# A hybrid DeltaNet and attention layer: inverse assembly read by ScalarE, layer norm in two VectorE operations a row, gate products in pieces, a later inverse norm

## The chip, the cores and the metric

The kernel runs on one core of one Trainium2 chip. The metric is the device time of one execution in microseconds (us). The engines are TensorE (PE in the rows; its weight loads PEld), VectorE (DVE), ScalarE (ACT), GpSimd (POOL) and SyncE (SP), which issues the DMAs. Each engine works through its own list of instructions in a fixed order and waits on semaphores for the others.

## What is computed

One layer over 2048 tokens of width 1024, float32, with 16 meta tokens in front. Cut to what matters here:

```python
q = l2_normalize(q) * (GDN_DK ** -0.5);  k = l2_normalize(k)
decay = exp(where(tri, g_cum[..., :, None] - g_cum[..., None, :], -inf))
lower = where(strict, einsum('bhnid,bhnjd->bhnij', k * beta, k) * decay, 0)
sol   = triangular_solve(lower + eye(CHUNK), rhs)       # chunks of 64 tokens, 8 heads
attn  = einsum('bhnid,bhnjd->bhnij', q, k) * decay
...                                                     # recurrence over chunks, gated norm
out   = (g_a * (y_a @ w_proj_a) + g_b * (y_b @ w_proj_b)) @ w_out
y     = (h2 - mean(h2)) * rsqrt(var(h2) + LN_EPS) * ln_w + ln_b     # h2 = DEEPNORM_ALPHA * h + out
```

A second branch, sliding-window attention, takes the same input; the change does not touch it.

## The kernel before

The 2048 tokens go in four blocks of 512. For each block the kernel projects the input with all weights, a unit of 16 or 24 matmuls 128x512 at a time (L296; weights as high and low parts wh, wl or wr). Between the units stand the small steps of the DeltaNet branch, in four groups g of two heads each, and then those of the attention branch. A Python scheduler writes this order out at build time: each step is a generator, a `yield` gives way to the next piece of matmuls, `yield 3` inside a background generator means that it goes on three such ticks later. So a different count of yields, or a line at another place, moves instructions in an engine's list, and nothing is reordered on the chip.

The steps of one group, in the names of the rows:

- `conv_unit`: ScalarE copies a projected unit (L681 to L686), VectorE applies a four-tap convolution (three SCALAR_TENSOR_TENSOR of 128x512, L689), ScalarE takes a tanh (L692), VectorE forms the SiLU (L694). This is done for k, q and v of two heads.
- `stage_b0`: GpSimd multiplies a triangle mask with the gate columns gh and gl (L729, one 128x1024 product each), TensorE sums them (L740, two matmuls for each head), ScalarE exponentiates (L741), GpSimd masks (L743). The result is E.
- `stage_b1`: VectorE forms the scalars of the keys (L777 to L781, 128x8) and the lower triangle LT (L784, eight operations reading PSUM). `inverse` then sends its diagonal blocks through DRAM (L798, L802), GpSimd solves them by substitution (62 short L810/L812), and two DMAs bring the result XT back (L818, L823).
- `stage_b2`: the inverse norm irk of the keys (`rsqrt_small` on sk, L160 to L166, and L837: 13 small VectorE operations), then attn = (k q) E (L842 on TensorE, L843 on VectorE) for two heads, the norms of q (L849), then v in token order, which ScalarE scales by irk (L859).
- `stage_c`: XT is transposed (XN, L875) and the inverse is assembled in two levels: L888 on TensorE, Y copied from PSUM (L893), L898/L900, copies into N64 and LT (L901, L904), L909.

At the end of a block, `project` adds the output projection to the residual; the layer norm of its four rows r0 to r3 (128 tokens each) falls into the start of the next block. `norm()` takes mean and inverse deviation for all four rows, then for each row one ScalarE operation (L1278, scale rs and bias nmr = -mean rs), one VectorE product with the weight (L1280), one GpSimd addition of the bias (L1282), and an output DMA on SP (L1284). The last block's rows go through `norm_row` instead. SP also issues the weight loads (L244), in its list's order.

Of the kernel before, what the change touches and what calls it, by code (L numbers as in the profile page):

```python
# [73 lines left out]
def hybrid_kernel(  # L74
# [47 lines left out]
    def g4(shape, dt=F32):  # L122
        return gp.tile(shape, dt, tag="g", name=nm("g"))
# [452 lines left out]
    def block(b, nextx):  # L576
# [145 lines left out]
        def stage_b0(g):  # L722

            d, h0 = gr[g], 2 * g
            yield from until(lambda: "gp" in gates)
            gts = []
            for part in gates["gp"]:
                gt = g4([P, 2, NC4, P], F32R)
                G.tensor_tensor(out=gt, in0=tri.unsqueeze(1).unsqueeze(1).to_broadcast([P, 2, NC4, P]),  # L729
                                in1=part[:, :, h0:h0 + 2].rearrange("p c h -> p h c").unsqueeze(3).to_broadcast([P, 2, NC4, P]), op=ALU.mult)  # L730
                gts.append(gt)
                yield

            def end():
                yield 3
                E = g4([P, 2, TB])
                for hh in range(2):
                    pm = bank()
                    for i, gt in enumerate(gts):
                        T.matmul(pm, strictr, gt[:, hh].rearrange("p c i -> p (c i)"), start=i == 0, stop=i == 1)  # L740
                    A.activation(E[:, hh, :], pm, AF.Exp)  # L741
                    yield 1
                    G.tensor_tensor(out=E[:, hh, :].rearrange("p (c i) -> p c i", c=NC4), in0=E[:, hh, :].rearrange("p (c i) -> p c i", c=NC4),  # L743
                                    in1=tri.unsqueeze(1).to_broadcast([P, NC4, P]), op=ALU.mult)
                d["E"] = E

            bg(end())
# [81 lines left out]
        def stage_b2(g):  # L829
# [2 lines left out]
            yield from until(lambda: ("ok", "qT", 1) in d)  # L832
            kT, qT, E, sk = d["kT"], d["qT"], d.pop("E"), d["sk"]
            sq = tiny([P, 2, NC4], "sq")
            irk = tiny([P, 2, NC4], "irk")
            rsqrt_small(irk, sk, [P, 2, NC4], "rs")
            V.tensor_tensor(out=irk, in0=irk, in1=sk, op=ALU.mult)  # L837
            attn = g4([P, 2, NC4, P])
            for hh in range(2):
                pq = bank()  # L840
                for c in range(NC4):
                    T.matmul(pq[:, c * P:(c + 1) * P], kT[:, hh, c * P:(c + 1) * P], qT[:, hh, c * P:(c + 1) * P], start=True, stop=True)  # L842
                V.tensor_tensor(out=attn[:, hh], in0=pq.rearrange("p (c i) -> p c i", c=NC4), in1=E[:, hh, :].rearrange("p (c i) -> p c i", c=NC4), op=ALU.mult)  # L843
                yield
                pq = bank()
                for c in range(NC4):
                    T.transpose(out=pq[:, c * P:(c + 1) * P], in_=qT[:, hh, c * P:(c + 1) * P], identity=ident)
                for c in range(NC4):
                    A.activation(junk, pq[:, c * P:(c + 1) * P], AF.Square, accum_out=sq[:, hh, c:c + 1])  # L849
                yield  # L850
            vtok = g4([P, 2, NC4, P])
            for hh in range(2):
                yield from until(lambda: ("ok", "vT", hh) in d)
# [13 lines left out]
        def stage_c(g):  # L867
# [22 lines left out]
            Y = tiny([P, 8, 32], "Y", 1)  # L890
            for s in range(2):
                bq = 64 * s + 32
                V.tensor_copy(Y[bq:bq + 32], py[bq:bq + 32, 0:256].rearrange("p (m i) -> p m i", m=8))  # L893
            yield
            px = bank()
            for m in range(8):
# [1 line left out]
                    T.matmul(px[a:a + 32, m * 32:m * 32 + 32], Y[bq:bq + 32, m, :], XT[bq:bq + 32, m, :],  # L898
                             start=True, stop=True, tile_position=(bq, a))
                T.matmul(px[32:64, m * 32:m * 32 + 32], XT[32:64, m, :], Y[32:64, m, :], start=True, stop=True, tile_position=(32, 32))  # L900
            V.tensor_copy(N64[32:64, :, 0:32], px[32:64, 0:256].rearrange("p (m i) -> p m i", m=8))  # L901
            for s in range(2):
                a, bq = 64 * s, 64 * s + 32
                A.activation(LT[a:a + 32, :, bq:bq + 32], px[a:a + 32, 0:256].rearrange("p (m i) -> p m i", m=8), AF.Copy)  # L904
# [341 lines left out]
        def project(nx):  # L1246
# [13 lines left out]
            def scale(n, mv):  # L1260

                var = tiny([P, n], "var")
                V.tensor_scalar(out=var, in0=mv[:, :, 1], scalar1=16.0 * LN_EPS, scalar2=None, op0=ALU.add)
                rs = tiny([P, n], "lrs")
                rsqrt_small(rs, var, [P, n], "ln")
                nmr = tiny([P, n], "nmr")
                V.scalar_tensor_tensor(out=nmr, in0=mv[:, :, 0], scalar=-1.0, in1=rs, op0=ALU.mult, op1=ALU.mult)
                return rs, nmr

            def norm():  # L1270
                lw, lb = norm_params()
                mv = tiny([P, NC4, 2], "mv")
                for c in range(NC4):
                    V.bn_aggr(out=mv[:, c, :], in_=bss[c])
                rs, nmr = scale(NC4, mv)
                for c in range(NC4):
                    yield 3
                    A.activation(xr[c], xr[c], AF.Identity, scale=rs[:, c:c + 1], bias=nmr[:, c:c + 1])  # L1278
                    yield 2
                    V.tensor_tensor(out=xr[c], in0=xr[c], in1=lw, op=ALU.mult)  # L1280
                    yield 1
                    G.tensor_tensor(out=xr[c], in0=xr[c], in1=lb, op=ALU.add)  # L1282
                    yield 2
                    SY.dma_start(out=out_[t0 + c * P:t0 + (c + 1) * P, :], in_=xr[c])  # L1284

            def norm_row(c, params):
                lw, lb = params
                mv = tiny([P, 1, 2], "mvr")
                V.bn_aggr(out=mv[:, 0, :], in_=bss[c])
                rs, nmr = scale(1, mv)  # L1290
                for h in range(2):
                    sl = slice(512 * h, 512 * h + 512)
                    A.activation(xr[c][:, sl], xr[c][:, sl], AF.Identity, scale=rs, bias=nmr)
# [192 lines left out]
```

## Time and profile before

| what | value |
|---|---|
| median of 3 runs | 2690.58 us (2689.68 to 2692.38) |
| the profiled execution | 2691.56 us, of which the profile's span is 2689.8 us |
| TensorE busy | 2611.2 us, 97% of the span |
| VectorE busy | 1623.8 us, 60% |
| ScalarE busy | 1220.4 us, 45% |
| GpSimd busy | 783.6 us, 29% |
| chain that ended last, by engine | PE 77%, DVE 12%, ACT 3%, POOL 3%, DMA 2% |

Times in the views run from the span's start. Block 1 begins near 734 us, block 2 near 1381, block 3 near 2029. The chain is followed back from the last instruction, at each step to what released it. An idle time of an engine is put down to the releaser that came last, in square brackets behind a row; "issue" means that the profile shows no releaser.

### The profile page before, as it was taken

The numbers are of one execution on the slowest core, as the hardware profiler recorded it, in microseconds if no ns is written. First come the engines' busy times: TensorE is split into PE (matmuls) and PEld (weight loads), VectorE is DVE, ScalarE is ACT, GpSimd is POOL, SyncE is SP. The second block draws the span as 40 slices with busy tenths as digits, with TensorE's granted clock in tenths as the row PEclk, the third lists the DMA queues.
The fourth block names the chain that finished last, engine by engine and source line by source line (L and its number), as shares of the span: only waits on it lengthen the run. The fifth ranks groups of instructions, "written<-read, shape, count | busy, mean of one in ns | idle before, by whom it ended". The sixth has DMA issues, their size and how long they took to land.

```text
span 2689.8 us, 44101 instructions
## 1 busy us (share of the span) xinstructions
PE 2611.2 (97%) x15308; PEld 2188.4 (81%) x15308; DVE 1623.8 (60%) x4080; ACT 1220.4 (45%) x3214; POOL 783.6 (29%) x1619
## 2 busy tenths in 40 slices
PE   8999999999999999999998999999999999999997
PEld 6777788888877888888887888888888788888885
DVE  6879768743475665762466564675347466476336
ACT  4555546542244544662234554565223455465322
POOL 1544324432055430111116433110103544111022
PEclk9999999999999999999999999999999999999999
DMA  7654556643664454764465445575357545467533
GB/s 245 210 171 159 189 184 187 202 163 99 200 230 141 145 174 142 207 194 146 151 214 178 140 144 171 170 214 174 117 165 232 169 140 152 154 194 213 162 97 128
DMA packets 243374, 461.64 MB, mean 172 GB/s; under 512 B 77992, under 2 KB 136000, under 8 KB 243152
## 3 DMA queue, kind: packets, MB, share of 16 engines
q1 hardware_dynamic: 243152, 458.82, 54.2%
q8 instruction: 122, 2.00, 0.3%
q14 instruction: 100, 0.82, 0.1%
HBM read 379.89 MB, written 78.82 MB: 171 GB/s over the span
## 4 chain that ended last, share of the span: by engine, by line
PE 77%; DVE 12%; ACT 3%; POOL 3%; DMA 2%; issue 2%; SPq 1%; DVEq 0%; ACTq 0%
PE acc L296 54%; DVE s L689 4%; PE ps L1108 2%; PE ps L1073 2%; POOL X L812 1%; POOL tm L810 1%; PE ps L960 1%; PE ps L939 1%; PE ps L928 1%; PE ps L947 1%; PE ps L949 1%; PE ps L1126 1%; PE acc L1367 1%; PE acc L1370 1%; PE acc L1369 1%
## 5 line engine op out<-in xcount | busy, mean ns | idle before, releaser
L296 PE MATMUL acc<-xh,wh 128*128 128x512 f32 x1800 | 740.6, 411 | 0.7 <-ACT wh L261 0.7
L296 PE MATMUL acc<-xl,wh 128*128 128x512 f32 x1800 | 711.2, 395 | 0.0
L296 PE MATMUL acc<-xh,wl 128*128 128x512 f32 x1800 | 479.1, 398 | 0.0
L296 PEld LDWEIGHTS acc<-xh,wh 128*128 128x128 f32 x1800 | 343.0, 191 | 61.4 <-ACT wh L261 1.0
L296 PEld LDWEIGHTS acc<-xl,wh 128*128 128x128 f32 x1800 | 343.6, 191 | 58.6
L296 PEld LDWEIGHTS acc<-xh,wl 128*128 128x128 f32 x1800 | 333.1, 190 | 67.8 <-issue 0.5
L261 ACT ACTIVATE wh<-wr 128x1024 fp32r<-128x1024 f32 (+1 forms) x245 | 258.0, 1053 | 277.6 <-PE acc L296 158.8
L689 DVE SCALAR_TENSOR_TENSOR s<-st,cw,s 128x512 f32<-128x512 f32 x288 | 252.4, 877 | 67.3 <-ACT st L684 59.9
L144 DVE TENSOR_TENSOR wl<-wr,wh 128x1024 fp32r<-128x1024 f32 (+2 forms) x125 | 165.9, 1327 | 157.3 <-ACT wh L261 138.3
L296 PE MATMUL acc<-y,wh 128*128 128x512 f32 x1024 | 250.1, 392 | 0.0
L810 POOL TENSOR_TENSOR tm<-X,g 128x60 f32<-128x60 f32 (+24 forms) x496 | 169.1, 341 | 265.5 <-DMA g<-d 229.3
L296 PEld LDWEIGHTS acc<-y,wh 128*128 128x128 f32 x1024 | 189.1, 188 | 37.3
L296 PE MATMUL acc<-xh,wr 128*128 128x512 f32 x624 | 210.2, 404 | 0.0
L1225 POOL TENSOR_TENSOR g<-g 128x512 f32<-128x512 f32 x32 | 69.9, 2184 | 432.7 <-DVE g L1218 432.7
L812 POOL TENSOR_TENSOR X<-X,tm 128x60 f32<-128x60 f32 (+24 forms) x496 | 178.9, 361 | 38.9
L1218 DVE SCALAR_TENSOR_TENSOR g<-g,acc 128x512 f32<-128x512 f32 x64 | 44.0, 688 | 203.1 <-PE acc L296 202.9
L1054 POOL TENSOR_TENSOR g<-mo,slp 128x32 f32<-128x32 f32 x128 | 41.1, 331 | 390.3 <-DVE mn L1075 364.5
L1110 ACT ACTIVATE s<-ps 104x512 fp32r<-104x512 f32 (+2 forms) x128 | 76.5, 597 | 146.3 <-PE ps L1108 145.3
L296 PEld LDWEIGHTS acc<-xh,wr 128*128 128x128 f32 x624 | 117.1, 190 | 23.3
L692 ACT ACTIVATE s<-s 128x512 f32<-128x512 f32 x96 | 60.4, 629 | 158.1 <-DVE s L689 158.1
L1209 ACT ACTIVATE g<-acc,bg__157 128x512 f32<-128x512 f32 x64 | 44.2, 690 | 190.2 <-PE acc L296 189.7
L296 PE MATMUL acc<-y,wl 128*128 128x512 f32 x512 | 129.2, 390 | 0.0
(329 smaller groups left out, 4768.5 us busy)
## 6 DMA issues: line engine op xcount, KB each, us to landing
wr<-in_wfm_dram SPq DMA_DIRECT2D x214, 512.0 KB
wl<-ws SPq DMA_DIRECT2D x165, 512.0 KB
wr<-ws SPq DMA_DIRECT2D x78, 512.0 KB
wh<-ws SPq DMA_DIRECT2D x75, 512.0 KB
ws<-wl SPq DMA_DIRECT2D x68, 512.0 KB
g<-kd SPq DMA_DIRECT2D x240, 96.0 KB
ws<-wh SPq DMA_DIRECT2D x38, 512.0 KB
wr<-in_wo_dram SPq DMA_DIRECT2D x32, 512.0 KB
```

Source lines behind the costliest of these rows:

```text
L144: eng.tensor_tensor(out=out_, in0=src, in1=f(hi), op=ALU.subtract)
L261: A.activation(hi, raw, AF.Copy)
L296: T.matmul(ps, w_[:, k, :], r_(k), start=(n == 0), stop=(n == 3 * NK - 1))
L689: V.scalar_tensor_tensor(out=acc, in0=st[:, 3 - d:TB + 3 - d], scalar=cw[:, s, 3 - d:4 - d], in1=acc, op0=ALU.mult, op1=ALU.add)
L692: A.activation(th, acc, AF.Tanh, scale=0.5)
L810: G.tensor_tensor(out=tm[:, :n, :r], in0=X[:, :n, j:j + 1].to_broadcast([P, n, r]), in1=L[:, j:j + 1, j + 1:].to_broadcast([P, n, r]), op= ...
L812: G.tensor_tensor(out=X[:, :n, j + 1:], in0=X[:, :n, j + 1:], in1=tm[:, :n, :r], op=ALU.add)
L1073: T.matmul(o_, d["q", rt][:, 2 * cp2 + ch], KX[:, l, ch, s:208], start=l == 0, stop=l == 1)
L1108: T.transpose(out=pT[0:kt, j * 256 + rt * P:j * 256 + rt * P + P], in_=Pt[:, ch, rt, s + j * kt:s + j * kt + kt], identity=ident)
L1110: A.activation(ph[0:kt], pT[0:kt], AF.Copy)
L1209: A.activation(gt_[u][:, br, :], ps, AF.Tanh, scale=0.5, bias=bg_[:, 8 * br + u:8 * br + u + 1])
L1225: G.tensor_tensor(out=m[:, u % 2, :], in0=t[:, 0, :], in1=t[:, 1, :], op=ALU.add)
```

## The change

Four edits:

1. `stage_b0`: each gate product of 128x1024 becomes four of 128x256 (one head, two of the four chunks).
2. `stage_b2`: the 13 operations of irk move from in front of the attn loop to behind it, in front of vtok.
3. `stage_c`: Y (two copies) and N64's lower block are copied out of PSUM by ScalarE instead of VectorE.
4. `norm()`: a row is now (x - mean) * lw and then x * rs + lb, two VectorE SCALAR_TENSOR_TENSOR of 128x1024; the ScalarE and GpSimd operations go, nmr is formed in `norm_row` only. The yields of a row were 3, 2, 1, 2 and are 1, 1, 1.

```diff
@@ stage_b0
-                G.tensor_tensor(out=gt, in0=tri.unsqueeze(1).unsqueeze(1).to_broadcast([P, 2, NC4, P]),
-                                in1=part[:, :, h0:h0 + 2].rearrange("p c h -> p h c").unsqueeze(3).to_broadcast([P, 2, NC4, P]), op=ALU.mult)
+                for hh in range(2):
+                    for c in range(0, NC4, 2):
+                        G.tensor_tensor(out=gt[:, hh, c:c + 2], in0=tri.unsqueeze(1).to_broadcast([P, 2, P]),
+                                        in1=part[:, c:c + 2, h0 + hh:h0 + hh + 1].to_broadcast([P, 2, P]), op=ALU.mult)
@@ stage_b2
-            irk = tiny([P, 2, NC4], "irk")
-            rsqrt_small(irk, sk, [P, 2, NC4], "rs")
-            V.tensor_tensor(out=irk, in0=irk, in1=sk, op=ALU.mult)
             attn = g4([P, 2, NC4, P])
...
+            irk = tiny([P, 2, NC4], "irk")
+            rsqrt_small(irk, sk, [P, 2, NC4], "rs")
+            V.tensor_tensor(out=irk, in0=irk, in1=sk, op=ALU.mult)
             vtok = g4([P, 2, NC4, P])
@@ stage_c
-                V.tensor_copy(Y[bq:bq + 32], py[bq:bq + 32, 0:256].rearrange("p (m i) -> p m i", m=8))
+                A.activation(Y[bq:bq + 32], py[bq:bq + 32, 0:256].rearrange("p (m i) -> p m i", m=8), AF.Copy)
...
-            V.tensor_copy(N64[32:64, :, 0:32], px[32:64, 0:256].rearrange("p (m i) -> p m i", m=8))
+            A.activation(N64[32:64, :, 0:32], px[32:64, 0:256].rearrange("p (m i) -> p m i", m=8), AF.Copy)
@@ norm
-                    yield 3
-                    A.activation(xr[c], xr[c], AF.Identity, scale=rs[:, c:c + 1], bias=nmr[:, c:c + 1])
-                    yield 2
-                    V.tensor_tensor(out=xr[c], in0=xr[c], in1=lw, op=ALU.mult)
                     yield 1
-                    G.tensor_tensor(out=xr[c], in0=xr[c], in1=lb, op=ALU.add)
-                    yield 2
+                    V.scalar_tensor_tensor(out=xr[c], in0=xr[c], scalar=mv[:, c, 0:1], in1=lw, op0=ALU.subtract, op1=ALU.mult)
+                    yield 1
+                    V.scalar_tensor_tensor(out=xr[c], in0=xr[c], scalar=rs[:, c:c + 1], in1=lb, op0=ALU.mult, op1=ALU.add)
+                    yield 1
                     SY.dma_start(out=out_[t0 + c * P:t0 + (c + 1) * P, :], in_=xr[c])
```

TensorE's list is the same, instruction for instruction. On VectorE, in group 0 of block 1, this stood from the triple L689 to the inverse norm and the attn products (L1280 is row r3 of the norm):

```order
L1280 TENSOR_TENSOR y_7685<-y_7685,y_8020 128x1024
L694 SCALAR_TENSOR_TENSOR g_8509<-s_8498,s_8455 128x512
L689 SCALAR_TENSOR_TENSOR s_8521<-st_8519,cw,s_8521 128x512 x3
L160 TENSOR_SCALAR rsi_8548<-sk_8340 128x8
...
L837 TENSOR_TENSOR irk_8546<-irk_8546,sk_8340 128x8
L843 TENSOR_TENSOR g_8563<-ps_8564,g_8391 128x512
L694 SCALAR_TENSOR_TENSOR g_8509<-s_8577,s_8521 128x512
L655 TENSOR_TENSOR s_8615<-acc_8535,s_8601 128x512
L843 TENSOR_TENSOR g_8563<-ps_8617,g_8391 128x512
```

Now, in the changed kernel (whose L842, L852 are L843, L837 of before):

```order
L694 SCALAR_TENSOR_TENSOR g_8538<-s_8525,s_8483 128x512
L689 SCALAR_TENSOR_TENSOR s_8553<-st_8551,cw,s_8553 128x512 x3
L842 TENSOR_TENSOR g_8577<-ps_8578,g_8421 128x512
L694 SCALAR_TENSOR_TENSOR g_8538<-s_8590,s_8553 128x512
L655 TENSOR_TENSOR s_8628<-acc_8566,s_8614 128x512
L842 TENSOR_TENSOR g_8577<-ps_8630,g_8421 128x512
L655 TENSOR_TENSOR s_8698<-acc_8640,s_8692 128x512
L160 TENSOR_SCALAR rsi_8702<-sk_8371 128x8
...
L852 TENSOR_TENSOR irk_8700<-irk_8700,sk_8371 128x8
```

The row of the norm is gone from here (all eight operations of the norm stand at the block's start), and both attn products stand ahead of the inverse norm.

On ScalarE, at the inverse assembly of the same group (N_275 is N64, L692 the tanh that waits for a triple L689):

```order
L884 ACTIVATE N_275_1550<-XN_8993 32x8x32
L692 ACTIVATE s_9036<-s_8985 128x512
L895 ACTIVATE Y_9055<-ps_9038 32x256 x2
L681 ACTIVATE st_9076<-acc_9015 128x512
L683 ACTIVATE s_9078<-acc_9015,cw 128x512
L684 ACTIVATE st_9076<-carry 128x3
L686 ACTIVATE carry<-st_9076 128x3
L903 ACTIVATE N_275_1550<-ps_9087 32x8x32
```

Y's two copies, which stood on VectorE behind the triple, now stand on ScalarE behind the tanh of the same triple.

On SP, at the start of block 1, before (y_7679 to y_7685 are the rows r0 to r3):

```order
L1284 DMA out_dram<-y_7679 128x1024
L244 DMA wr_8190<-ws_602 128x1024
L244 DMA wr_8191<-ws_603 128x1024
L624 DMA vd<-s_8141 128x512
...
L624 DMA vd<-s_8147 128x512
L244 DMA wh_8273<-ws_696 128x1024
L244 DMA wl_8274<-ws_697 128x1024
L1284 DMA out_dram<-y_7681 128x1024
```

and now (y_7703 to y_7709 are r0 to r3):

```order
L1282 DMA out_dram<-y_7707 128x1024
L244 DMA wr_8218<-ws_608 128x1024
L244 DMA wr_8219<-ws_609 128x1024
L1282 DMA out_dram<-y_7709 128x1024
L624 DMA vd<-s_8166 128x512
...
L624 DMA vd<-s_8172 128x512
L244 DMA wh_8300<-ws_702 128x1024
L244 DMA wl_8301<-ws_703 128x1024
```

The output of all four rows now stands ahead of the value stores (L624) and of the weight pair behind them.

## Rows read from the trace of the kernel before

**Rows 1.** The page, busy us (share of the span) and instructions of each engine.

```profile
PE 2611.2 (97%) x15308; PEld 2188.4 (81%) x15308; DVE 1623.8 (60%) x4080; ACT 1220.4 (45%) x3214; POOL 783.6 (29%) x1619
```

**Rows 2.** The waits of PE: who waited, for whom, us, times, longest.

```profile
PE ps L898 <- issue: 12.5, 3, 4.6
...
PE ps L740 <- DVE g L843: 9.1, 3, 3.1
```

**Rows 3.** Timeline of PE: start, us, line, [idle before it <- releaser]; blocks 0, 1.

```profile
114.98 0.66 PE L760 MATMUL ps<-cm,g 128*128 128x128 f32 x4 [0.95 <-DVE g L694]
...
762.40 0.62 PE L740 MATMUL ps<-g,strictr 128*128 128x512 f32 x2
...
788.87 1.21 PE L740 MATMUL ps<-g,strictr 128*128 128x512 f32 x2 [3.08 <-DVE g L843]
...
831.68 0.67 PE L898 MATMUL ps<-XT,Y 32*32 32x32 f32 x3 [4.26 <-issue]
```

**Rows 4.** Stretches: us, busy time of each engine (instructions), PEclk, DMA share, GB/s.

```profile
788.80:792.30 3.50, 3.43 (x8) 2.70 (x9) 1.82 (x4) 0.65 (x2) 3.14 (x6) 0.52 1.03 411
829.90:836.70 6.80, 4.88 (x57) 3.94 (x58) 6.06 (x14) 3.37 (x8) 0.51 (x2) 0.50 0.59 161
115.00:118.40 3.40, 3.40 (x17) 2.88 (x18) 3.19 (x10) 3.27 (x14) 0.71 (x3) 1.00 0.54 168
```

**Rows 5.** Timeline of DVE in group 0 of block 1, at the attn products.

```profile
781.48 4.28 DVE L689 SCALAR_TENSOR_TENSOR s<-st,cw,s 128x512 f32<-128x512 f32 x3
785.67 0.22 DVE L160 TENSOR_SCALAR rsi<-sk 128x8 int32<-128x8 int32 x1
...
788.13 0.68 DVE L843 TENSOR_TENSOR g<-ps,g 128x512 f32<-128x512 f32 x1
788.74 0.68 DVE L694 SCALAR_TENSOR_TENSOR g<-s,s 128x512 f32<-128x512 f32 x1
```

**Rows 6.** Timeline of POOL in the same stretch.

```profile
780.84 2.78 POOL L1282 TENSOR_TENSOR y<-y,y 128x1024 f32<-128x1024 f32 x1 [6.42 <-DVE y L1280]
...
784.63 0.43 POOL L810 TENSOR_TENSOR tm<-X,g 128x31 f32<-128x31 f32 x1 [0.21 <-DMA g<-d]
...
788.93 1.64 POOL L743 TENSOR_TENSOR g<-g,cm 128x512 f32<-128x512 f32 x1 [1.13 <-ACT g L741]
```

**Rows 7.** Timeline of DVE at the inverse assembly of group 0 of block 1.

```profile
822.42 0.45 DVE L875 STREAM_TRANSPOSE XN<-XT 128x256 f32<-128x256 f32 x1 [3.92 <-DMA XT<-d]
...
823.20 1.54 DVE L779 TENSOR_TENSOR cj<-cj,gm4be 128x8 f32<-128x8 f32 x1
824.77 1.84 DVE L780 TENSOR_SCALAR ncj<-cj 128x8 f32<-128x8 f32 x1
...
828.81 2.32 DVE L689 SCALAR_TENSOR_TENSOR s<-st,cw,s 128x512 f32<-128x512 f32 x3
831.16 0.88 DVE L893 COPY Y<-ps 32x256 f32<-32x256 f32 x2
```

**Rows 8.** Timeline of DVE at the start of block 1.

```profile
735.45 1.23 DVE L1280 TENSOR_TENSOR y<-y,y 128x1024 f32<-128x1024 f32 x1 [1.31 <-ACT y L1278]
738.76 0.42 DVE L611 COPY ba<-acc 128x16 f32<-128x16 f32 x3 [2.09 <-PE acc L598]
...
756.24 2.08 DVE L694 SCALAR_TENSOR_TENSOR g<-s,s 128x512 f32<-128x512 f32 x1 [0.30 <-ACT s L692]
```

**Rows 9.** Timeline of SP at the start of block 1: a weight load.

```profile
748.25 1.00 SPq L244 DMA_DIRECT2D wh<-ws  x1
```

**Rows 10.** Timeline of POOL at 822: the first gate product of a later group.

```profile
822.76 1.94 POOL L729 TENSOR_TENSOR g<-cm,gh 128x1024 fp32r<-128x1024 f32 x1
```

**Rows 11.** The page's costliest groups: busy us, mean ns | idle before, releaser.

```profile
L810 POOL TENSOR_TENSOR tm<-X,g 128x60 f32<-128x60 f32 (+24 forms) x496 | 169.1, 341 | 265.5 <-DMA g<-d 229.3
```

**Rows 12.** Timeline of ACT at the inverse assembly of block 1.

```profile
831.17 0.63 ACT L692 ACTIVATE s<-s 128x512 f32<-128x512 f32 x1 [7.42 <-DVE s L689]
```

**Rows 13.** Timeline of ACT in block 0: v scaled by the inverse norm.

```profile
95.05 1.15 ACT L859 ACTIVATE g<-ps,irk 128x128 f32<-128x128 f32 x4
```

More of the change, by code (lines that the diff above doesn't have):

```diff
@@ L1265, in scale @@
                 rsqrt_small(rs, var, [P, n], "ln")
-                nmr = tiny([P, n], "nmr")
-                V.scalar_tensor_tensor(out=nmr, in0=mv[:, :, 0], scalar=-1.0, in1=rs, op0=ALU.mult, op1=ALU.mult)
-                return rs, nmr
+                return rs
             def norm():
@@ L1274, in norm @@
                     V.bn_aggr(out=mv[:, c, :], in_=bss[c])
-                rs, nmr = scale(NC4, mv)
+                rs = scale(NC4, mv)
                 for c in range(NC4):
-                    yield 3
-                    A.activation(xr[c], xr[c], AF.Identity, scale=rs[:, c:c + 1], bias=nmr[:, c:c + 1])
-                    yield 2
-                    V.tensor_tensor(out=xr[c], in0=xr[c], in1=lw, op=ALU.mult)
                     yield 1
-                    G.tensor_tensor(out=xr[c], in0=xr[c], in1=lb, op=ALU.add)
-                    yield 2
+                    V.scalar_tensor_tensor(out=xr[c], in0=xr[c], scalar=mv[:, c, 0:1], in1=lw, op0=ALU.subtract, op1=ALU.mult)
+                    yield 1
+                    V.scalar_tensor_tensor(out=xr[c], in0=xr[c], scalar=rs[:, c:c + 1], in1=lb, op0=ALU.mult, op1=ALU.add)
+                    yield 1
                     SY.dma_start(out=out_[t0 + c * P:t0 + (c + 1) * P, :], in_=xr[c])
@@ L1289, in norm_row @@
                 V.bn_aggr(out=mv[:, 0, :], in_=bss[c])
-                rs, nmr = scale(1, mv)
+                rs = scale(1, mv)
+                nmr = tiny([P, 1], "nmr")
+                V.scalar_tensor_tensor(out=nmr, in0=mv[:, :, 0], scalar=-1.0, in1=rs, op0=ALU.mult, op1=ALU.mult)
                 for h in range(2):
```

## The prediction

> **What bounds the kernel now.** The page's busy line comes first: TensorE is busy for 2611.2 of 2689.8 us [rows 1], so the other engines matter only where TensorE waits for them, some 60 us in all. The view of TensorE's waits says for whom. Of its long rows, L898 (12.5 us in 3 waits) and L740 (9.1 us in 3) [rows 2] repeat once in each of blocks 1, 2 and 3, in the places that this change edits; the others lie at the start, in block 0 or in the attention half. In block 1 they are L740 at 788.87, after 3.08 us, and L898 at 831.68, after 4.26 us [rows 3]. A wait also costs clock: in the 3.5 us behind the first the granted clock was 0.52, in the 6.8 us around the second 0.50, the 1.2 GHz level, while behind a wait of 0.95 us it stayed at 1.00 [rows 4]. The L740 wait so costs 3.08 + 0.48 x 3.5 = 4.8 us. But gaining those 4.8 us is worth nothing by itself if L898 still begins when it did. So I followed the chain of waits back from L898, and it does not run over TensorE: DVE L689 (781), ACT, POOL L743 (789), POOL's substitution chain L810/L812 to 814.8, two DMAs, XN, the five small operations L777 to L781, L784, L689, Y. **What decides blocks 1 to 3 is how much earlier Y is ready**, until TensorE itself becomes the bound, at 831.68 - 4.26 - 4.8 = 822.6, 9.1 us earlier.
>
> **The norm.** Row r3's L1280 and L1282 leave the front of that chain. The POOL add L1282 lies at 780.84 for 2.78 us, and the three L689 at 781.48 take 4.28 us beside it [rows 5, 6] where a clean triple, at 828.81, takes 2.32 [rows 7]: 2.0 us of that is the POOL add. With L843 no longer behind the inverse norm either, L740's wait goes. Its 4.8 us bring TensorE to L888 at about 819.0, where XN is then late. POOL's next L743 waited 1.13 us for ACT and started at 788.93; the substitution step before it (its first instruction is at 784.63 [rows 6]) was done at 787.8. ACT and DVE being early, L743 starts behind that step, and its DMA comes up to 0.5 us sooner, because the gate pieces let L777 in: the chain begins its rest 1.1 to 1.7 us earlier.
>
> What the norm adds is eight VectorE operations 128x1024 at the block's start, ahead of the gates. Such an operation with a scalar has no row; L1280 takes 1.23 us [rows 8], and at 128x512 a SCALAR_TENSOR_TENSOR like L694 (0.68 us at 788.74) takes as long as a TENSOR_TENSOR (0.68 at 788.13 [rows 5]). Bounds: 1.2 us, and two thirds of a triple of L689, 1.55; I take 1.2. Four of them fill the idle 1.31 us, the place of one L1280 and the 2.09 us in front of L611 at 738.76 [rows 8]. The third row pushes L621 back by 2.0 us and the gates, with half of the fourth row, by 3.1. The other half takes the place of row r1's L1280. The second triple of L689 then loses its POOL add, 2.0 us as at 781, so the gate column gh is about 1.0 us late, at 756.6.
>
> Its DMA: on SP, out row r3 now stands in front of the four value stores L624 and of the weight pair that was issued at 748.25 [rows 9]. r3 is normalised about 753.6, and behind the stores the pair goes at about 755.7, 7 us late. Its matmuls stand right behind L740 at 762.40 [rows 3], another 7 us later. I cost this at nothing; the bounds are 0 and, if the pair needed 9 us, 2.
>
> **The pieces.** L729, 1.94 us for 128x1024 [rows 10], becomes four of 128x256. Bounds for one: a quarter, 0.48, and a quarter plus the 0.34 mean of the small POOL product L810 [rows 11], 0.82; nearest is the quarter, I take 0.55, or 4.4 us for eight. Next to L729 the eight-element L779 took 1.54 us and L780 1.84 [rows 7], each ending with a POOL product, and L694 at 756.24 took 2.08 for 0.68 [rows 8]: VectorE and POOL take turns, instruction by instruction. So with pieces each small operation waits for at most 0.55: L777 to L781 shrink by some 2.0 us. The turns cut the other way too: VectorE gets in between the pieces, and the product as a whole ends later. After XN it then lasts until L689, a triple that was clean at 828.81: one or two pieces fall into it, +0.8 us (0 to 1.65).
>
> The Trainium skill, "SBUF — State Buffer", section "Who interferes with whom", says that a VectorE instruction with two SBUF inputs contends with a GpSimd one that reads SBUF, and that whoever issues first keeps the shared ports for the whole instruction. The elongated rows agree; by that rule alone, a VectorE operation could meet four times as many POOL instructions, which is the second rival's mechanism below.
>
> At the block's start the same turns cost something. gh, 1.0 us late, gives a first piece at 756.9; then L694, three L689 and the pieces alternate, so the sixth piece (which the second L740 needs) ends at 756.9 + 6 x 0.55 + 0.7 + 3 x 0.75 = 763.15, where TensorE asks at about 762.6 [rows 3]: a new wait of 0.5 us, without loss of clock by [rows 4]. It moves the units behind it and so VectorE's input; the chain hides half of it: +0.25.
>
> **Y and N64 on ScalarE.** Y was two copies of together 0.88 us directly behind L689 [rows 7]. On ScalarE they stand behind L692, which starts when L689 is done (831.17, 0.63 us [rows 12]): +0.55 (0 to 0.7). N64 costs nothing: ScalarE was idle then.
>
> **The inverse norm.** 13 operations from 785.67 to 788.13, 2.46 us [rows 5], go behind both L843. In blocks 1 to 3 VectorE has idle time there and nothing is late. In block 0, group 0 it has none: L859 at 95.05 [rows 13] must wait for them, the key-tile copies and L261 queued behind it on ScalarE with it, and through DVE L689 the L760 that waits 0.95 us at 114.98 [rows 3]. Bounds 0 and +2.5; against it, the pieces shorten a wait at 55 and N64 one at 143, about 1.6 us at most. I take +0.8.
>
> **Sum.** Per block 1 to 3: -1.4 (chain) -2.0 (small operations) +0.8 (L689 meets pieces) +0.55 (Y) +0.25 (rest of the new L740 wait that the chain does not hide) = -1.8 us at L898, where all behind it is TensorE-bound. Three blocks -5.4, block 0 +0.8, nothing in the last block's tail: -4.6 us. The profiled execution took 2691.56 us (span 2689.8 and 1.8 around it), 0.98 over the median of 2690.58: 2691.56 - 4.6 - 0.98 = **2686.0 us**.
>
> **The rivals.**
> 1. The chain gives all it can: pieces of 0.48, none left at L689, Y hidden, -3.7 us a block, block 0 even: 2690.6 - 11.1 = 2679.5. For it: TensorE has 9.1 us of room there. Against it: ScalarE's order puts Y behind L692.
> 2. Contention only moves: each L689 of the triple behind XN waits for a piece of 0.55 to 0.8. It takes back 1.65 to 2.0 of the 2.0 us, and with Y's 0.55 only 0.3 us a block are left: 2690.6 - 0.9 + 0.8 = 2690.5. For it: the triples with POOL beside them [rows 5]. Against it: only some of eight pieces are left by then.
> 3. Slower: the second L740 of each block's first group. If a piece costs 0.82 us, the sixth ends 1.6 us later than above, the wait is over 2 us, and the 1.2 GHz level takes a further 1.7 us as behind L740 at 788.87. It decides from about 1 us of wait on, since 0.95 left the clock alone. Then 3.7 us a block arrive at the chain in place of 0.5; nothing is won at L898 but +1.4 to +2: 2690.6 + 5.5 + 0.8 = 2697. An SP queue that hands the weight pair over too late, behind out row r3, would cost at the same place.
>
> **How the numbers follow.** Forecast 0.45 (2682.5 to 2689.5), rival 1 0.20, rival 2 0.17, rival 3 0.15, others 0.03. About 0.2% (5.4 us) is what a measurement of this kernel can tell from no change; the bound is 2685.2. Faster: 0.18 of the forecast, rival 1 and a bit, 0.40. Within: 0.27 of the forecast and most of rival 2, 0.42. Slower: rival 3 and others, 0.18. The range leaves out the ends of rivals 1 and 3: 2678 to 2696.
>
> **What would show it.** Right: L740's wait on DVE L843 gone; a wait at L888 of about 2 us in front of XN; L898 at about 829.9; L777 to L781 within 2 us; Y's first copy behind L692; pieces near 0.55 us; a wait of about 0.5 us at L740 near 762.6. Wrong: an L898 that starts before 828 or after 831, a granted clock of 0.5 behind L740 at 762, TensorE waiting for weights behind out row r3, or time gained outside these places.

## The result, and the profile after

The changed kernel takes 2667.24 us (median of 4 runs, 2665.94 to 2668.51) against 2691.48 us of the kernel before, run beside it: a ratio of 0.9909, interval 0.9897 to 0.992. It is **24 us faster, where 4.6 us were forecast**; the time lies 11 us below the range. The sign of the forecast was right, its size wrong by a factor of five. The profiled execution has a span of 2664.2 us, 25.6 less than before.

The page of the changed kernel, its busy line (us, share of the span, instructions):

```profile
PE 2600.1 (98%) x15308; PEld 2180.1 (82%) x15308; DVE 1587.5 (60%) x4041; ACT 1223.7 (46%) x3250; POOL 765.8 (29%) x1703
```

TensorE is 11 us less busy with the same instructions [rows 1], since it ran less often at half clock (granted clock 0.994 on average, 0.987 before); the rest is waits that went. Its waits now (who, for whom: us, times, longest; line numbers are up by two where code was added above):

```profile
PE ps L900 <- ACT Y L895: 10.2, 8, 3.7
...
PE ps L859 <- ACT g L861: 5.5, 2, 2.8
...
PE ps L890 <- DVE sk L779: 1.3, 1, 1.3
```

L740's wait [rows 2] is gone. L900, the L898 of before, still waits some 10 us [rows 2], but it comes 5 to 7 us earlier in each block. L859 in block 0 waits for v and did not before.

TensorE's list did not change, so each of its 15308 instructions can be set beside its counterpart. L636, early in each block's DeltaNet part, begins 5.3 us earlier in block 1 (744.59 for 749.87), 12.4 in block 2, 19.6 in block 3; the last matmul 25.6. **So block 0 gave 5.3 us, block 1 7.1, block 2 7.2, block 3 with the tail 6.0.** These are one execution of each kernel, and block 0 alone varies: two runs below whose lists are the same in block 0 (irk_first and y_hold) differ there by 5.2 us. What follows counts times in block 1 from L636, which takes out what earlier blocks gave:

| block 1, us behind L636 (lines of the kernel before) | before | after | difference |
|---|---|---|---|
| first keys' operation on sk (L777) | 22.69 | 20.63 | -2.06 |
| LT ready for its DMA (L784 done) | 27.51 | 24.65 | -2.86 |
| substitution begins (L810) | 34.76 | 31.91 | -2.85 |
| GpSimd's next L743 inside it | 39.05 | 34.73 | -4.32 |
| XN (L875) | 72.55 | 67.39 | -5.16 |
| second group's L784 begins | 76.86 | 69.10 | -7.76 |
| triple L689 behind it done | 81.26 | 73.97 | -7.29 |
| L898 | 81.81 | 75.08 | -6.73 |

VectorE at the last rows of this table, in the changed kernel (start us, us, line), beside [rows 7]:

```profile
811.98 0.45 DVE L877 STREAM_TRANSPOSE XN<-XT 128x256 f32<-128x256 f32 x1 [3.58 <-DMA XT<-d]
...
812.75 0.24 DVE L781 TENSOR_TENSOR cj<-cj,gm4be 128x8 f32<-128x8 f32 x1
813.02 0.54 DVE L782 TENSOR_SCALAR ncj<-cj 128x8 f32<-128x8 f32 x1
...
815.77 2.79 DVE L689 SCALAR_TENSOR_TENSOR s<-st,cw,s 128x512 f32<-128x512 f32 x3
```

and ScalarE and TensorE there:

```profile
818.59 0.63 ACT L692 ACTIVATE s<-s 128x512 f32<-128x512 f32 x1 [5.24 <-DVE s L689]
819.24 0.78 ACT L895 ACTIVATE Y<-ps 32x256 f32<-32x256 f32 x2
```

```profile
819.67 0.24 PE L900 MATMUL ps<-XT,Y 32*32 32x32 f32 x2 [2.31 <-ACT Y L895]
```

These last steps went as the forecast had them: the small operations 0.24 and 0.54 us for 1.54 and 1.84, the triple 2.79 for 2.32, Y behind L692. What it missed lies above them in the table, in the front of the chain. There L694 and the first operation on sk stood beside a product before, and now stand beside pieces. Before, and then the changed kernel:

```profile
771.01 1.62 DVE L694 SCALAR_TENSOR_TENSOR g<-s,s 128x512 f32<-128x512 f32 x1 [0.70 <-ACT s L692]
772.56 1.88 DVE L777 TENSOR_SCALAR sk<-sk 128x8 f32<-128x8 f32 x1
```

```profile
764.39 0.90 DVE L694 SCALAR_TENSOR_TENSOR g<-s,s 128x512 f32<-128x512 f32 x1 [0.70 <-ACT s L692]
765.22 0.58 DVE L779 TENSOR_SCALAR sk<-sk 128x8 f32<-128x8 f32 x1
```

GpSimd in the changed kernel, beside [rows 6]: the substitution's first operation, and the L743 of before, which no longer waits.

```profile
776.50 0.64 POOL L812 TENSOR_TENSOR tm<-X,g 128x31 f32<-128x31 f32 x1 [7.50 <-DMA g<-d]
...
779.31 1.30 POOL L745 TENSOR_TENSOR g<-g,cm 128x512 f32<-128x512 f32 x1
```

### The profile page after: what moved, and what is told of

Its sections match the earlier page's. It is cut to its first block, busy times and chain, and to the rows that moved or that the text cites. A ratio compares the mean times of both kernels' runs of the same rounds, so it can differ in the third digit from the quotient of the medians.

```text
span 2664.2 us, 44181 instructions
## 1 busy us (share of the span) xinstructions
PE 2600.1 (98%) x15308; PEld 2180.1 (82%) x15308; DVE 1587.5 (60%) x4041; ACT 1223.7 (46%) x3250; POOL 765.8 (29%) x1703
## 4 chain that ended last, share of the span: by engine, by line
PE 81%; DVE 10%; DMA 3%; POOL 2%; ACT 2%; issue 1%; SPq 1%; DVEq 0%; POOLq 0%; ACTq 0%
PE acc L296 57%; PE ps L1110 2%; DVE s L689 2%; PE ps L1075 2%; PE ps L962 1%; PE ps L941 1%; PE ps L949 1%; PE ps L951 1%; PE ps L930 1%; PE ps L1128 1%; PE acc L1367 1%; PE acc L1370 1%; PE acc L1369 1%; PE ps L841 1%; POOL X L814 1%
## 5 line engine op out<-in xcount | busy, mean ns | idle before, releaser
L689 DVE SCALAR_TENSOR_TENSOR s<-st,cw,s 128x512 f32<-128x512 f32 x288 | 233.4, 810 | 66.6 <-ACT st L684 59.5
L814 POOL TENSOR_TENSOR X<-X,tm 128x60 f32<-128x60 f32 (+24 forms) x496 | 165.4, 333 | 38.9
L731 POOL TENSOR_TENSOR g<-cm,gh 128x256 fp32r<-128x256 f32 x64 | 50.7, 822 | 257.8 <-DVE gh L643 211.5
```

The costliest lines, as they stand in the source:

```text
L689: V.scalar_tensor_tensor(out=acc, in0=st[:, 3 - d:TB + 3 - d], scalar=cw[:, s, 3 - d:4 - d], in1=acc, op0=ALU.mult, op1=ALU.add)
L731: G.tensor_tensor(out=gt[:, hh, c:c + 2], in0=tri.unsqueeze(1).to_broadcast([P, 2, P]), in1=part[:, c:c + 2, h0 + hh:h0 + hh + 1].to_broad ...
L814: G.tensor_tensor(out=X[:, :n, j + 1:], in0=X[:, :n, j + 1:], in1=tm[:, :n, :r], op=ALU.add)
```

## The experiments

Two theories. **"Turns"**: what counts is how long one GpSimd instruction keeps a VectorE operation waiting, all along the chain to L898, so the pieces carry the gain. **"Adds"**: the norm's GpSimd additions beside the triples L689 were what held the chain. All times are medians; the kernel before, run beside each set, had 2690.7, 2690.7, 2691.3 and 2692.3 us.

### Each edit alone

The pieces alone:

```diff
-                G.tensor_tensor(out=gt, in0=tri..., in1=part[:, :, h0:h0 + 2]..., op=ALU.mult)
+                for hh in range(2):
+                    for c in range(0, NC4, 2):
+                        G.tensor_tensor(out=gt[:, hh, c:c + 2], ...)
```

> The kernel before with the gate products in four pieces and nothing else. Theory 'turns': VectorE and GpSimd take turns instruction by instruction, and a whole product of 1.9 us holds up L689, L694 and L777 ahead of the substitution chain as well as L777 to L781 behind it; then pieces alone bring L898 forward by about 5 us in each of blocks 1 to 3 and about 3 us in block 0: 2691.5 - 18 = 2673 us (2670 to 2678). Theory 'adds': the GpSimd additions of the norm are what held the chain; then pieces alone give only the 2 us of L777 to L781 a block: 2685 us (2683 to 2688).

2678.27 us, ratio 0.9947 (0.9932 to 0.9962). Faster by 12.4 us: nearer to "turns" than to "adds", and just outside the range of "turns". L898 came 2.9, 3.5 and 4.0 us earlier in blocks 1 to 3, where "turns" had about 5.

The norm alone:

```diff
-                    A.activation(xr[c], ...); V.tensor_tensor(..., in1=lw); G.tensor_tensor(..., in1=lb)
+                    V.scalar_tensor_tensor(..., in1=lw, ...); V.scalar_tensor_tensor(..., in1=lb, ...)
```

> The kernel before with the norm as two VectorE operations a row and nothing else. Theory 'adds': the triples L689 beside the additions fall from 4.2 to 2.3 us, the chain comes 4 to 5 us earlier a block: 2677 us (2674 to 2681). Theory 'turns': the product of 1.9 us still holds the chain's front, and 1.5 to 2 us a block are won: 2686 us (2684 to 2689).

2693.67 us, ratio 1.0009 (1.0 to 1.0019): nothing won, both theories wrong. VectorE at the block's start shows why. L694 and the triple still stand beside a whole product, as in [rows 8], and all of it comes 0.7 us later behind L636, after the norm's eight operations:

```profile
759.72 2.08 DVE L694 SCALAR_TENSOR_TENSOR g<-s,s 128x512 f32<-128x512 f32 x1 [0.30 <-ACT s L692]
761.73 3.98 DVE L689 SCALAR_TENSOR_TENSOR s<-st,cw,s 128x512 f32<-128x512 f32 x3
...
776.07 1.88 DVE L777 TENSOR_SCALAR sk<-sk 128x8 f32<-128x8 f32 x1
```

The inverse norm alone (its three lines moved behind the attn loop):

```diff
-            irk = ...; rsqrt_small(irk, sk, ...); V.tensor_tensor(out=irk, in0=irk, in1=sk, op=ALU.mult)
             attn = g4([P, 2, NC4, P])
...
+            irk = ...; rsqrt_small(irk, sk, ...); V.tensor_tensor(out=irk, in0=irk, in1=sk, op=ALU.mult)
             vtok = g4([P, 2, NC4, P])
```

> The kernel before with the keys' inverse norm behind the attn products and nothing else. Both theories: in blocks 1 to 3 the wait at L740 shrinks from 3.1 to about 0.6 us, and TensorE waits that much longer at L898, since the chain behind Y does not pass L740; nothing is won there. In block 0 v waits for the inverse norm: about 2.6 us at 115 and new waits of about 2.7 us at 168 and 249, partly taken back later: 2694 us (2691 to 2699). If instead L740's wait was on the path, blocks 1 to 3 win 2.5 us each: 2686 us.

2694.38 us, ratio 1.0013 (1.0004 to 1.0023), as expected. TensorE's waits in it: the L740 wait of 3.1 us a block is down to 0.6, and what it gave is waited for again, at L888, in front of XN; v waits in block 0.

```profile
PE ps L888 <- DVE sk L777: 12.1, 3, 4.3
...
PE ps L857 <- ACT g L859: 5.7, 2, 2.9
```

Y and N64 on ScalarE alone:

```diff
-                V.tensor_copy(Y[bq:bq + 32], ...)
+                A.activation(Y[bq:bq + 32], ..., AF.Copy)
...
-            V.tensor_copy(N64[32:64, :, 0:32], ...)
+            A.activation(N64[32:64, :, 0:32], ..., AF.Copy)
```

> The kernel before with Y and N64 copied by ScalarE and nothing else. Both theories: L898 comes 0.55 us later in blocks 1 to 3, since Y stands behind L692 (+1.7 in all), and block 0 wins 1 to 3 us at the inverse assembly near 142: 2690 us (2688 to 2693).

2686.77 us, ratio 0.9983 (0.9973 to 0.9992): 3.9 us faster, more than expected. The gain lies at block 0's inverse assembly: between 130 and 155 TensorE's list wins 6.3 us, and blocks 1 to 3 together none. Before, TensorE waited 1.97 us at L415, and the granted clock over the next 7 us was 0.63; without Y and N64 on VectorE that wait is gone and the clock stays at 1.00. In the traces of all six kernels here that copy Y and N64 on VectorE TensorE waits 0.7 to 2.0 us at L415, in the ten that copy them on ScalarE at most 0.3. The wait and the stretch before, then the stretch in this run (columns as in [rows 4]):

```profile
141.95 0.39 PE L415 MATMUL ps<-cm,mkm 128*16 128x128 f32 x2 [1.97 <-DVE mkm L411]
```

```profile
142.00:149.00 7.00, 6.42 (x36) 4.78 (x37) 4.90 (x9) 5.82 (x18) 0.00 (x0) 0.63 1.01 321
```

```profile
140.00:147.00 7.00, 7.00 (x70) 5.20 (x70) 5.35 (x13) 4.25 (x15) 0.00 (x0) 1.00 0.99 317
```

The four differences sum to -8.7 us (-12.4, +3.0, +3.7, -3.9 against the before beside them); together the edits give -24. So they do not add.

### Each edit left out of the changed kernel

Each of these is the changed kernel with one hunk of the diff taken back.

```diff
+                G.tensor_tensor(out=gt, in0=tri..., in1=part[:, :, h0:h0 + 2]..., op=ALU.mult)
-                for hh in range(2):
-                    for c in range(0, NC4, 2):
-                        G.tensor_tensor(out=gt[:, hh, c:c + 2], ...)
```

> The changed kernel with the gate products whole again. By the runs of the single edits, L898 stands 81.8 us behind L636 before, 75.1 after, 78.9 with pieces alone, 81.5 with the norm alone (block 1). Theory 'coupled': whole products hold L689, L694 and L777 at the block's start, so the norm's and the inverse norm's gain behind them does not arrive; L898 near 81 to 82, block 0 about -3: 2688 us (2685 to 2692). Theory 'norm on its own': the two VectorE operations carry what is missing in the sum of the single edits: 2678 us.

2692.24 us, ratio 1.0002 (0.9993 to 1.0012), at the upper end of "coupled". **Without the pieces the other three edits are worth nothing.** L898 stands 82.6 us behind L636 in block 1, 81.8 before.

```diff
+                    A.activation(xr[c], ...); V.tensor_tensor(..., in1=lw); G.tensor_tensor(..., in1=lb)
-                    V.scalar_tensor_tensor(..., in1=lw, ...); V.scalar_tensor_tensor(..., in1=lb, ...)
```

> The changed kernel with the old norm (ScalarE, VectorE, GpSimd). Theory 'coupled': with pieces alone, GpSimd's L743 in the substitution chain still waited 1.1 us for ScalarE, behind the triple L689 beside the GpSimd addition; so L898 stays at about 78.5 to 79 where it is 75.1, +3 to +4 us a block: 2677 us (2674 to 2680). Theory 'the additions do not matter': 2668 us.

2673.74 us, ratio 0.9934 (0.9919 to 0.9949): 6.5 us slower than the changed kernel, as "coupled" had it, though the time lies just below its range. L898 stands 4.7, 4.1 and 1.6 us later behind L636 in blocks 1 to 3. The row expected is there: r3's addition lies beside the triple in front of the substitution chain, and GpSimd's L743 (L745 here) waits for ScalarE again, as in [rows 6].

```profile
772.81 4.28 DVE L689 SCALAR_TENSOR_TENSOR s<-st,cw,s 128x512 f32<-128x512 f32 x3
```

```profile
780.27 1.28 POOL L745 TENSOR_TENSOR g<-g,cm 128x512 f32<-128x512 f32 x1 [0.74 <-ACT g L743]
```

```diff
+            irk = ...; rsqrt_small(irk, sk, ...); V.tensor_tensor(out=irk, ...)
             attn = g4([P, 2, NC4, P])
...
-            irk = ...; rsqrt_small(irk, sk, ...); V.tensor_tensor(out=irk, ...)
             vtok = g4([P, 2, NC4, P])
```

> The changed kernel with the inverse norm in front of the attn products again. Block 0 loses its waits for v at 113, 168 and 249 (8 us, of which about 3 come back as other waits): -5 us. In blocks 1 to 3, theory 'L740 counts': the second L740 waits again, GpSimd's second L743 comes about 1.5 us later, and L898 with it: +4.5 in all, 2667 us (2665 to 2669). Theory 'L740 is beside the path': nothing is lost there, 2662 us (2660 to 2664).

2667.94 us, ratio 0.9913 (0.9898 to 0.9928): 0.7 us from the changed kernel, no difference that these runs resolve. Block 0 was 2.6 us better and blocks 1 to 3 together about 4 worse in the profiled execution, near "L740 counts"; L898 behind L636 is 0.25 to 0.6 us later a block, which places a third of it.

```diff
+                V.tensor_copy(Y[bq:bq + 32], ...)
-                A.activation(Y[bq:bq + 32], ..., AF.Copy)
...
+            V.tensor_copy(N64[32:64, :, 0:32], ...)
-            A.activation(N64[32:64, :, 0:32], ..., AF.Copy)
```

> The changed kernel with Y and N64 copied by VectorE again. From the chain: L898 0.55 us earlier a block (Y directly behind L689), and block 0 without what the single edit won there (about 4 us): 2669 us (2667 to 2672). If ScalarE's copies only cost: 2665 us.

2671.04 us, ratio 0.9924 (0.9909 to 0.9938): 3.8 us slower by the medians, near what was expected, but the two sets of runs overlap (2666.99 to 2674.74 here), so the size is uncertain. The profiled execution, the slowest of the four, loses 7.8 us in block 0. In blocks 1 to 3 L898 is 0.45 to 0.7 us earlier, the price of Y behind L692.

### The norm needs the pieces, and nothing else

The kernel before with those two edits:

```diff
+                        G.tensor_tensor(out=gt[:, hh, c:c + 2], ...)
...
+                    V.scalar_tensor_tensor(..., in1=lw, ...); V.scalar_tensor_tensor(..., in1=lb, ...)
```

> The kernel before with the pieces and the norm in two VectorE operations, the inverse norm and Y as before. Theory 'the norm pays once pieces let it' (alone it cost 3 us, its removal from the changed kernel cost 6.5): 2672 us (2669 to 2675), E1 (GpSimd's L743 inside the substitution chain) at 34.8 us behind L636. Theory 'the inverse norm has to leave L843 too': E1 near 37 as with pieces alone, 2678 us (2676 to 2681).

2669.28 us, ratio 0.991 (0.9895 to 0.9925), as the first theory said: -23 of the 24 us, by the medians. L743 stands 34.79 us behind L636, where pieces alone had 37.21 and the norm alone 38.37, and it does not wait:

```profile
781.50 1.29 POOL L745 TENSOR_TENSOR g<-g,cm 128x512 f32<-128x512 f32 x1
```

With pieces alone, r3's addition still holds the triple (4.27 us) in front of L743, which waits 1.13 us. With the norm alone L743 does not wait either, but whole products hold everything ahead of it: the substitution begins 35.61 us behind L636, with both edits 31.96. Only both together clear the line.

### The size of a piece

The changed kernel with two, then eight pieces a product:

```diff
-                    for c in range(0, NC4, 2):
-                        G.tensor_tensor(out=gt[:, hh, c:c + 2], in0=tri.unsqueeze(1).to_broadcast([P, 2, P]), ...)
+                    for c in range(0, NC4, 4):
+                        G.tensor_tensor(out=gt[:, hh, c:c + 4], in0=tri.unsqueeze(1).to_broadcast([P, 4, P]), ...)
```

> The changed kernel with two pieces of 128x512 a gate product instead of four of 128x256. Theory 'turns': a small VectorE operation beside a product waits for the piece in progress, so from XN to L784, 4.3 us before and 1.7 with quarters, takes about 2.6 with halves, and the first group's sk operations likewise; L898 1 to 2 us later a block: 2671 us (2669 to 2675). Theory 'any cut will do' (what counts is that VectorE gets in at all): 2667 us.

2680.99 us, ratio 0.9963 (0.995 to 0.9975): 10 us slower than "turns" said, and 14 than "any cut will do".

```diff
-                    for c in range(0, NC4, 2):
-                        G.tensor_tensor(out=gt[:, hh, c:c + 2], in0=tri.unsqueeze(1).to_broadcast([P, 2, P]), ...)
+                    for c in range(0, NC4):
+                        G.tensor_tensor(out=gt[:, hh, c:c + 1], in0=tri.unsqueeze(1).to_broadcast([P, 1, P]), ...)
```

> The changed kernel with eight pieces of 128x128 a gate product. Theory 'turns': the wait of one operation is halved again, about 0.3 us less in each of the two places, but the product lasts longer, by a fixed cost a piece and by more turns with the triples L689, which take 0.5 us more; the gate products of a block's first group end later than 13.7 us behind L636, where L742 asks at 14.4, and TensorE may wait: 2668 us (2664 to 2674). Theory 'the shorter the better': 2663 us.

2660.23 us, ratio 0.9884 (0.9869 to 0.9898), better by 7 us than quarters, and below both theories. So the size matters far more than "turns" with my prices had it. The traces give the prices. VectorE beside the first products of block 1, with halves and then with eighths, to be read beside 2.08 in [rows 8] for L694 with whole products:

```profile
753.22 1.22 DVE L694 SCALAR_TENSOR_TENSOR g<-s,s 128x512 f32<-128x512 f32 x1 [0.29 <-ACT s L692]
754.37 4.44 DVE L689 SCALAR_TENSOR_TENSOR s<-st,cw,s 128x512 f32<-128x512 f32 x3
...
769.56 0.74 DVE L781 TENSOR_TENSOR cj<-cj,gm4be 128x8 f32<-128x8 f32 x1
770.34 0.97 DVE L782 TENSOR_SCALAR ncj<-cj 128x8 f32<-128x8 f32 x1
```

```profile
749.19 0.93 DVE L694 SCALAR_TENSOR_TENSOR g<-s,s 128x512 f32<-128x512 f32 x1 [0.30 <-ACT s L692]
750.34 2.55 DVE L689 SCALAR_TENSOR_TENSOR s<-st,cw,s 128x512 f32<-128x512 f32 x3 [0.23 <-ACT st L684]
...
763.39 0.26 DVE L782 TENSOR_SCALAR ncj<-cj 128x8 f32<-128x8 f32 x1
```

And the second L689 out of such a triple (clean: 0.75), with quarters, halves and eighths:

```profile
753.59 0.99 DVE L689 SCALAR_TENSOR_TENSOR s<-st,cw,s 128x512 f32<-128x512 f32 x1
```

```profile
755.93 1.42 DVE L689 SCALAR_TENSOR_TENSOR s<-st,cw,s 128x512 f32<-128x512 f32 x1
```

```profile
751.32 0.77 DVE L689 SCALAR_TENSOR_TENSOR s<-st,cw,s 128x512 f32<-128x512 f32 x1
```

Undisturbed, a piece takes in these traces 0.40 us (128x128), 0.61 (128x256), 1.06 (128x512), 1.92 (whole). An L689 directly behind another let one piece in and lost 0.67 us to a half, 0.24 to a quarter and 0.02 to an eighth: **each time about 0.4 us less than the piece takes.** So here the loss falls faster than the piece's length, and it is near nothing at 128x128. (L694, which comes upon a piece under way, still lost 0.25 us to an eighth.) With halves each of the three L689 loses its turn (4.44 us, worse than the 3.98 beside two whole products, where only the first met one); LT is therefore done 27.4 us behind L636 in block 1, as with whole products (27.5; quarters 24.65), which is why halves win so little.

The 7 us of the eighths are another matter. Beside the changed kernel, blocks 1 and 2 win nothing (+0.3 and -0.1 us); block 0 wins 2.5 us and block 3 with the tail 4.3. LT is done 0.8 us earlier in block 1, but GpSimd's L743 waits again, for ScalarE, whose operations in front of it had waited 1.13 us for TensorE's L846; XN comes 0.8 us later:

```profile
774.61 0.28 ACT L848 ACTIVATE junk<-ps 128x128 f32<-128x128 f32 x1 [1.13 <-PE ps L846]
```

```profile
777.23 1.29 POOL L745 TENSOR_TENSOR g<-g,cm 128x512 f32<-128x512 f32 x1 [1.01 <-ACT g L743]
```

With quarters L743 came only 0.25 us behind ScalarE's result, so the chain had little more to win up to there. In block 3 the substitution, late with quarters (33.4 us behind L636), begins at 31.6.

The Trainium skill, "SBUF — State Buffer", section "Who interferes with whom", gives the shared ports to whoever issues first for the whole instruction; it says so of VectorE's two-port modes, and of an instruction with two SBUF inputs, such as L689, only that it contends with GpSimd's reads. The runs agree that turns are taken instruction by instruction, but a turn cost VectorE clearly less than the GpSimd instruction's recorded time (0.24 us of 0.61).

### Where the inverse norm hurts, and Y ahead of L692

```diff
+            if first:
+                irk = ...; rsqrt_small(irk, sk, ...); V.tensor_tensor(out=irk, ...)
             attn = g4([P, 2, NC4, P])
...
+            if not first:
                 irk = ...; rsqrt_small(irk, sk, ...); V.tensor_tensor(out=irk, ...)
```

> The changed kernel with the inverse norm in front of the attn products in block 0 only, behind them in blocks 1 to 3. Both theories: blocks 1 to 3 as in the changed kernel, block 0 without the waits for v at 168 and 249 and with 1 us in place of 3.5 at 113: 2662 us (2660 to 2664).

2664.11 us, ratio 0.9898 (0.9883 to 0.9913): 3 us better than the changed kernel by the medians; the two sets of runs lie 0.3 us apart at their nearest, so it is likely better, by little, and just above what was expected. Where is not shown: in the profiled execution, the slowest of the four, block 0 is 0.5 us longer than in the changed kernel's. The waits for v at 168 and 249 are gone, but one at 280 grew from 2.5 to 5.6 us.

On top of that, the tanh L692 that meets the inverse assembly is issued one tick later; in the lists only three pairs of rows change, Y and L692 on ScalarE in the first groups of blocks 1 to 3.

```diff
             A.activation(N64[32:64, :, 32:64], XN[32:64], AF.Copy)
+            state["hold"] = not first
             yield
...
                 A.activation(Y[bq:bq + 32], ..., AF.Copy)
+            state["hold"] = False
...
                 yield CONV[1]
+                while state.get("hold"):
+                    yield 1
                 th = s2([P, TB])
```

> The kernel with the inverse norm early in block 0, and in blocks 1 to 3 the tanh L692 behind Y's two copies on ScalarE instead of ahead of them; nothing else moves in any list. Theory 'Y waits for L692': L898 waits 2.5, 2.5 and 3.7 us because Y stands behind a tanh that waits for L689; with the two exchanged TensorE does not wait there and keeps its clock: -8.7 us, and some -1.7 a block for the half clock behind the wait: 2664 - 8.7 - 5 = 2650 us (2648 to 2656). Theory 'the chain ends elsewhere' (N64, LT or L689 itself hold the next step): 2661 to 2664 us.

2652.17 us, ratio 0.9852 (0.9838 to 0.9867), as expected: 12 us by the medians from three exchanged pairs. Of the 16 us between the two profiled executions blocks 1 to 3 hold 11.0; the other 5.2 lie in block 0, where the lists are the same. Y is copied at 809.82, L692 (L694 here) runs at 814.16, and TensorE reaches L898 (L909 here) at 812.64 without a wait; the clock behind it is 1.00, where the changed kernel had 0.76:

```profile
809.82 0.78 ACT L903 ACTIVATE Y<-ps 32x256 f32<-32x256 f32 x2 [0.95 <-PE ps L898]
814.16 0.63 ACT L694 ACTIVATE s<-s 128x512 f32<-128x512 f32 x1 [3.56 <-DVE s L689]
```

```profile
812.64 0.22 PE L909 MATMUL ps<-XT,Y 32*32 32x32 f32 x2
```

```profile
810.00:817.00 7.00, 6.51 (x75) 4.86 (x74) 5.59 (x12) 3.31 (x9) 4.38 (x6) 1.00 0.61 212
```

```profile
817.50:824.50 7.00, 4.67 (x58) 3.70 (x59) 3.97 (x6) 4.61 (x11) 1.31 (x2) 0.76 0.56 140
```

The first stretch is that of this run, the second that of the changed kernel.

Last, the same with eight pieces:

```diff
-                    for c in range(0, NC4, 2):
-                        G.tensor_tensor(out=gt[:, hh, c:c + 2], ...)
+                    for c in range(0, NC4):
+                        G.tensor_tensor(out=gt[:, hh, c:c + 1], ...)
```

> The kernel with Y ahead of L692 and the inverse norm early in block 0, with eight pieces of 128x128 a product in place of four. Theory 'TensorE is now the bound in blocks 1 and 2' (L898 without a wait there): only block 0 and block 3 win from shorter pieces, 2648 us (2646 to 2651). Theory 'shorter pieces win everywhere': the 7 us of the changed kernel again, 2645 us. If the eighths end too late for L742: 2654 us.

**2648.59 us, ratio 0.9837 (0.9821 to 0.9854): the best version, 19 us under the changed kernel.** The eighths now win 3.6 us instead of 7, as the first theory had it. In blocks 1 and 2 TensorE does not wait at L898 in either version, and by TensorE's list they win nothing there (0.0 and 0.2 us); block 3 with the tail wins 3.0. Block 0 is 1.4 us longer in this execution, within what it varies by.

## Why the prediction was wrong

**Right.** That L740's own wait is off the path (alone, the inverse norm won nothing), and that Y's readiness at L898 sets blocks 1 to 3. The last terms of the sum measured close to the forecast: small operations -2.6 us (forecast -2.0), L689 meeting pieces +0.47 (+0.8), Y behind L692 +0.56 (+0.55). A piece takes 0.61 us (0.55 taken), a norm operation 1.28 (1.2 taken), gh came 0.7 us late (1.0). No wait arose at L742 near 757, and none for weights behind out row r3. So the term of +0.25 for L740 measured nothing. Nor was there the wait of 2 us at L888 in front of XN (only 1.3 us in block 3): XN came earlier still.

**Wrong: the term "chain", -1.4 us a block, measured -5.2 in block 1** (XN behind L636). Three things were mis-sized or left out, all at its front.

1. The block's first triple and the pieces were made to take turns at full price, so that the triple would end where it did before (762.1). It lost 0.24 us a turn, not 0.55, and ended 1.3 us earlier; the later triple, L694 and L777 stand behind it through ScalarE, and moved by the same.
2. L694 and L777 beside the next products (771 to 774) take 0.90 and 0.58 us in place of 1.62 and 1.88. The prediction let in "up to 0.5 us" for this whole stretch. With point 1, LT leaves for its DMA 2.86 us earlier.
3. As forecast, the triple at 781 lost its addition, and GpSimd's L743 no longer waited for ScalarE: that is the 1.1 us of the sum. But the substitution in front of L743 was let begin at most 0.5 us earlier, and it began 2.85 us earlier, as LT did. With its first steps, 0.3 us shorter, L743 came 4.3 us earlier, and XN 5.2.

So the sum costed the stage in which the last wait ends, and counted little upstream, where the same contention sat on the same chain. Rival 1 had the sign but was built from the same terms, with -3.7 us a block; L898 moved by 6.7, 6.6 and 4.9. The bound worked out from TensorE alone, 9.1 us, was not broken; with Y ahead of L692 and no wait left at L898 (y_hold), L898 moved by 9.06 in block 1.

**Wrong: block 0, forecast +0.8 us, measured -5.3 in the profiled executions.** How much of this is the change is open, since block 0 differs by as much between executions of the same lists. The inverse norm cost more than its bound of 2.5: 3.7 us in all as a single edit by the medians, and TensorE's list loses 4.2 us between 105 and 122 in the changed kernel. Underestimated was what stood against it, as the clock was left out of it: at 55 the wait fell from 3.84 us to 1.90 (52.98 in the changed kernel), and the clock stayed at 1.00 over the 3.4 us behind, where it had been 0.51; at 142 the wait of 1.97 went, with 0.63 over 7 us. The forecast had 1.6 us for the two; by TensorE's list they gave about 3.4 us (50 to 60) and 6.3 (130 to 155), of which later waits took a part back.

**The clock.** Rival 3 took a wait of about 1 us as the length that decides, from one wait of 0.95. The traces don't bear that out. Before, the clock stayed at 1.00 behind a wait of 1.81 us (L947 at 183.15) and was 0.57 behind one of 1.77 (L960 at 344.74). Behind the same L760 it was 1.00 after 1.90 us in the changed kernel and 0.58 after 1.90 with pieces alone. So the length of a wait alone does not tell what it costs in clock.

**The norm** was costed as a gain of its own in blocks 1 to 3. Alone it was none, and with whole products the three other edits together were none. That the terms add was assumed and never argued.

**Rival 3** asked for a wait of over 1 us at the second L740; there was none, since the pieces end earlier by point 1. **Rival 2** had the triple behind XN lose 1.65 us or more to pieces; it lost 0.47, but 2.1 with halves at the block's start: the mechanism exists, at twice the size of piece. (Its own terms leave 0.6 us a block or more, not the 0.3 that it states.)

What stays open, beside block 0: block 3 won less at L898 (4.9 us). Its LT was ready at the same time as in blocks 1 and 2, but the substitution began 1.5 us later, behind a DMA; why that DMA took longer was not tried.

## What to carry to other kernels

When the last wait hangs on a chain over several engines, follow it back to where it enters the stretch and look for the same contention there, before pricing the end of it; in block 1 three quarters of the gain at L898 were ahead of XN. Edits that shorten the same chain don't add: price them together, in the order of the chain, and test one with the other left out. Once a chain sets the time, look at what stands ahead of its steps in each in-order list; exchanging Y with a tanh that waited for something else was worth half as much as the whole change.

## What the runs showed that was not expected

- An L689 directly behind another, taking turns with GpSimd pieces, lost about 0.4 us less a turn than the piece's own time (0.67 of 1.06, 0.24 of 0.61, 0.02 of 0.40). So cutting a product into pieces of 128x128 (0.40 us) left a triple L689 at 2.55 us, clean 2.32, while halves made it 4.44, worse than the whole product's 3.98.
- A SCALAR_TENSOR_TENSOR 128x1024 with both tensors in SBUF took 1.28 us in each of the 24 operations of the norm, where the TENSOR_TENSOR of that size took 1.22.
- The granted clock stayed at 1.00 behind a wait of 1.90 us at 53, and was 0.51 behind one of 3.84 us at the same place before; but behind a wait of 1.90 us at that place with pieces alone it was 0.58:

```profile
52.48 0.66 PE L762 MATMUL ps<-cm,g 128*128 128x128 f32 x4 [1.90 <-DVE g L694]
```

```profile
52.50:55.90 3.40, 3.40 (x11) 2.78 (x12) 3.22 (x5) 3.27 (x17) 1.96 (x2) 0.58 0.63 260
```
